# Pairing the two DMA queues of an HBM-to-HBM shift on the same rows instead of on diagonal quadrants

## The chip, the cores and the metric

One core of a Trainium2 chip. The metric is the device time in microseconds. Executions of the kernel before agree within some 0.2% on one chip. Kernels are compared only within the same rounds.

## The reference

```python
def setup_inputs():
    return {"x": np.random.randn(8192, 8192).astype(np.float32)}

def reference(x):
    return np.fft.ifftshift(x)
```

For even sizes this swaps the quadrants: `out[r, c] = x[(r + 4096) % 8192, (c + 4096) % 8192]`. 268.44 MB are read from HBM (the memory outside the core) and as many written to it; nothing is computed. A row is 32 KiB, a half row 16 KiB.

## The kernel before

```python
STEP = 8
# ... R, C = 8192; hr = hc = 4096
dims = [[STEP * C, hr // STEP], [1, hc]]          # 512 half rows, every eighth row
for c in range(STEP):
    for col in (0, hc):
        for eng, r0, h in ((nc.sync, 0, col), (nc.scalar, hr, hc - col)):
            eng.dma_start(
                out=bass.AP(out.tensor, out.offset + (r0 + c) * C + h, dims),
                in_=bass.AP(x.tensor, x.offset + (hr - r0 + c) * C + hc - h, dims),
            )
```

32 DMAs of 8 MiB, 16 on each of two queues, straight from HBM to HBM. At any time sync and scalar work in diagonal quadrants. The order on each queue is that of the program; the waits are in the prediction.

Of the kernel before, what the change touches and what calls it, by code (L numbers as in the profile page):

```python
# [1 line left out]

# [4 lines left out]


STEP = 8  # L10


@with_exitstack
def kernel(
    ctx: ExitStack,
    tc: tile.TileContext,
    x: bass.AP,
    out: bass.AP,
):



    nc = tc.nc

    R, C = x.shape
    hr = R // 2
    hc = C // 2

    dims = [[STEP * C, hr // STEP], [1, hc]]
    for c in range(STEP):  # L30
        for col in (0, hc):
            for eng, r0, h in ((nc.sync, 0, col), (nc.scalar, hr, hc - col)):
                eng.dma_start(
                    out=bass.AP(out.tensor, out.offset + (r0 + c) * C + h, dims),
                    in_=bass.AP(x.tensor, x.offset + (hr - r0 + c) * C + hc - h, dims),
                )


# [1 line left out]
_INS = ['x']  # L40
_OUTS = [((8192, 8192), 'float32')]


def kernel(**inputs):
    import numpy as _np
    import concourse.bacc as _bacc
    import concourse.tile as _tile
    from concourse import mybir as _mybir
    from concourse.bass_utils import run_bass_kernel_spmd as _run

    nc = _bacc.Bacc("TRN2", target_bir_lowering=False, num_devices=1)  # L51
    arrays, args = {}, []
    for name in _INS:
        a = _np.ascontiguousarray(inputs[name])
        if a.dtype.kind in "iu":
            a = a.astype(_np.int64)
        arrays[f"in_{name}_dram"] = a
        args.append(nc.dram_tensor(f"in_{name}_dram", a.shape, _mybir.dt.from_np(a.dtype), kind="ExternalInput").ap())
    for i, (shape, dtype) in enumerate(_OUTS):
        dt = _mybir.dt.from_np(_np.dtype(dtype))  # L60
        args.append(nc.dram_tensor(f"out_{i}_dram", shape, dt, kind="ExternalOutput").ap())
    with _tile.TileContext(nc) as tc:
        kernel(tc, *args)
    r = _run(nc, [arrays], core_ids=[0])
    got = tuple(r.results[0][f"out_{i}_dram"] for i in range(len(_OUTS)))
    return got[0]
```

## Time and profile before

| | before |
|---|---|
| median of the three runs | 822.29 us |
| mean / median packet | 801 / 773 ns |
| packets at the floor (up to 615 ns) | 26.2% |
| packets over 1,000 ns | 14.6% |
| lead of sync's queue over scalar's, mean and 5 to 95% (20 to 760 us) | 3.4 rounds, 2.6 to 3.9 |

A packet is one entry of the trace's packet records, here one half row. The last four rows are worked out from these records, which hold queue, start, duration and bytes of each packet. A "round" is 16 packets of one queue, on average one for each engine, and the lead is the number of packets started on sync's queue less those on scalar's, over 16. The page itself is read in the prediction. One more view belongs to it, the copy's line with its two issuing queues (ns that the issue instruction took, minimum, median and maximum; then first and last start in us):

```profile
L33 ACTq DMA_DIRECT2D out_dram<-in_x_dram x16: 518/42177/48098, 0.7 to 618.8; - x16
L33 SPq DMA_DIRECT2D out_dram<-in_x_dram x16: 511/41599/47782, 0.7 to 613.7; - x16
```

An issue instruction of 42 us looks busy. But the first three on each queue took 0.6 to 0.9 us in the trace, and only the fourth 43 us (sync) and 48 us (scalar). So I read the long ones as waiting for room behind DMAs that are already queued; no view names this wait.

### The profile page before, as it was taken

How to read it: one execution, taken by the hardware profiler on the slowest of the kernel's cores; microseconds unless marked ns; L12 is line 12 of the kernel's file. 1: busy time of each engine (PE TensorE's matmuls, PEld its weight loads, DVE VectorE, ACT ScalarE, POOL GpSimd, SP SyncE). 2: the span in 40 equal slices, each digit the busy share in tenths (PEclk: the TensorE clock that was granted, in tenths of full speed). 3: DMA queues.
4: the chain of work that ended last, by engine and by line, in shares of the span. 5: the costliest groups of instructions: out<-in, count | busy, mean ns of one | idle time of the engine just before them, and what ended most of it. 6: DMA issues, size and time to landing. Idle time of an engine off the chain costs nothing. (4 is left out here: it accounts for less than half of the span.)

```text
span 821.3 us, 77 instructions
## 1 busy us (share of the span) xinstructions
POOL 0.2 (0%) x4
## 2 busy tenths in 40 slices
POOL 0000000000000000000000000000000000000000
DMA  9999999999999999999999999999999999999998
GB/s 304 325 328 333 326 325 330 321 329 330 325 330 330 327 328 333 329 330 330 328 328 327 334 325 330 326 326 328 331 329 330 326 332 326 328 324 333 326 328 298
DMA packets 16896, 268.44 MB, mean 327 GB/s; under 512 B 512, under 2 KB 512, under 8 KB 512
## 3 DMA queue, kind: packets, MB, share of 16 engines
q1 hardware_dynamic: 8448, 134.22, 50.2%
q10 hardware_dynamic: 8448, 134.22, 49.7%
HBM read 268.44 MB, written 268.44 MB: 654 GB/s over the span
## 5 line engine op out<-in xcount | busy, mean ns | idle before, releaser
L51 POOL MEMSET const-bfloat16-1.0<- 128x1 bf16 x1 | 0.1, 103 | 0.0
L51 POOL MEMSET const-uint8-127<- 128x1 uint8 x1 | 0.1, 102 | 0.0
L51 POOL MEMSET const-float32-0.0<- 128x1 f32 x1 | 0.1, 99 | 0.2 <-issue 0.2
L51 POOL MEMSET const-float32-1.0<- 128x1 f32 x1 | 0.1, 99 | 0.0
## 6 DMA issues: line engine op xcount, KB each, us to landing
out_dram<-in_x_dram ACTq DMA_DIRECT2D x16, 8192.0 KB, 204.3
out_dram<-in_x_dram SPq DMA_DIRECT2D x16, 8192.0 KB, 204.1
```

The costliest lines, as they stand in the source:

```text
L51: nc = _bacc.Bacc("TRN2", target_bir_lowering=False, num_devices=1)
```

## The change

The intent: let both queues work on the two column halves of the same rows at the same time, so that what they touch lies side by side, 16 KiB apart.

```diff
-    for c in range(STEP):
-        for col in (0, hc):
-            for eng, r0, h in ((nc.sync, 0, col), (nc.scalar, hr, hc - col)):
+    for r0 in (0, hr):
+        for c in range(STEP):
+            for eng, h in ((nc.sync, 0), (nc.scalar, hc)):
                 eng.dma_start(
                     out=bass.AP(out.tensor, out.offset + (r0 + c) * C + h, dims),
                     in_=bass.AP(x.tensor, x.offset + (hr - r0 + c) * C + hc - h, dims),
```

## The prediction

> **What bounds the kernel now.** I read the page from the top: engines first, then the slices, then the DMA queues, then the issues.
>
> ```profile
> span 821.3 us, 77 instructions
> ...
> POOL 0.2 (0%) x4
> ...
> DMA  9999999999999999999999999999999999999998
> GB/s 304 325 328 333 326 325 330 321 329 330 325 330 330 327 328 333 329 330 330 328 328 327 334 325 330 326 326 328 331 329 330 326 332 326 328 324 333 326 328 298
> DMA packets 16896, 268.44 MB, mean 327 GB/s; under 512 B 512, under 2 KB 512, under 8 KB 512
> ...
> q1 hardware_dynamic: 8448, 134.22, 50.2%
> q10 hardware_dynamic: 8448, 134.22, 49.7%
> HBM read 268.44 MB, written 268.44 MB: 654 GB/s over the span
> ...
> out_dram<-in_x_dram ACTq DMA_DIRECT2D x16, 8192.0 KB, 204.3
> out_dram<-in_x_dram SPq DMA_DIRECT2D x16, 8192.0 KB, 204.1
> ```
>
> No compute engine works: 0.2 us on GpSimd in the whole span. All 16 DMA engines are full in every slice and the rate is flat, 321 to 334 GB/s between the first and last slice. The two queues have the same bytes and together take 99.9% of the engines' time. So the span is moved bytes over a sustained rate. The start and the end hold little:
>
> ```profile
> 0.00:20.00 20.00, 0.20 (x4) 1.00 0.91 301
> 20.00:200.00 180.00, 0.00 (x0) 1.00 1.00 328
> 200.00:400.00 200.00, 0.00 (x0) 1.00 1.00 329
> 400.00:600.00 200.00, 0.00 (x0) 1.00 1.00 328
> 600.00:800.00 200.00, 0.00 (x0) 1.00 1.01 328
> 800.00:821.00 21.00, 0.00 (x0) 1.00 0.92 304
> ```
>
> (Columns: stretch, length, GpSimd, clock, DMA share, GB/s.) At 328 GB/s all 268.44 MB would take 818.4 us, so the ends cost about 3 us.
>
> The next question is what one packet costs. The trace's packet records hold 16,384 data packets of 16,384 bytes, each one half row, so 1,024 on each of the 16 engines. Their mean is 801 ns: 1,024 x 801 ns = 820 us, which is the span. The shortest is 608 ns, and 26% lie within 615 ns; the median is about 775 and 15% take over 1,000. So 611 ns (26.8 GB/s an engine, 429 over sixteen) is what a packet costs when nothing stands in its way, and if all packets were like that the span would be 1,024 x 611 = 626 us. The other 190 ns of the mean packet are waiting outside the engine, and the memory is the only shared thing left: read and written together it carries 654 GB/s.
>
> Last, the issue side, because a queue that ran dry would look like slow packets.
>
> ```profile
> SPq L62 <- DMA out_dram<-in_x_dram: 167.2, 2, 118.8
> SPq L33 <- DMA out_dram<-in_x_dram: 133.8, 12, 50.6
> ```
>
> Sync waits at the copy's line 12 times: from its fifth DMA on, each waits for the one four places earlier (eight completion semaphores, four a queue). This costs nothing: a DMA lands 204 us after its issue while one lands per queue every 51 us, so four are always queued and the engines stay full.
>
> **What the Trainium skill says.** (1) "DMA: Bandwidth & Descriptors", section "Issuing engines are not separate DMA queues": DMAs from any issuing engine run on the same 16 engines and interleave. The section "Queues, rings and completion order" adds that an engine goes round its queues by packet. The trace agrees: 50.2 against 49.7%, and the two queues' packet counts stay within four rounds of 16 packets of each other all along. (2) "HBM Reference", "Specifications (TRN2)": about 716 GB/s for a domain of two cores. With 654 GB/s of reads and writes the trace stands at 91% of that, if both tensors lie in one domain, which no view here shows. (3) "DMA: Bandwidth & Descriptors", "Latency and other measured facts", on row pitch at large powers of two: copies between HBM tensors fall to 207 GB/s a direction at a pitch of 512 KiB and to 103 at 4 MiB. Here the pitch within a DMA is 8 rows x 32 KiB = 256 KiB and the trace has 327, so this DMA shape isn't hit that hard; but the table says that the placement of concurrent streams can matter a lot.
>
> **The change, part by part.** *Removed and added instructions:* none. On each engine the order and the waits of the changed program compare as the same: 16 DMAs a queue, each 512 rows of 4,096 floats, first four without a wait, the rest behind the one four places earlier. Cost: 0. *Packets:* 16,384 data packets of 16 KiB as before, the same alignment and pitch. Cost: 0. *Bytes:* the same 268.44 MB each way. Cost: 0. *What moves:* the addresses that the two queues have in work together. Before, sync and scalar sat in diagonal quadrants: different row halves and different column halves, on both the read and the write side, 128 MiB plus or minus 16 KiB apart. After, sync writes the left and scalar the right half of the same output rows, from the two halves of the same input rows, nominally 16 KiB apart. For the first half of the time all reads are from the lower half of x and all writes go to the upper half of out, then the reverse.
>
> So the whole effect must come through the 190 ns of waiting per packet. Two readings say that address relation matters little. First, before already contains variants: even DMAs of a queue have the one sign of the column offset and odd DMAs the other, and c runs from 0 to 7. Grouped in starting order, the mean packet of a DMA is 785 to 823 ns on q1 (sync, the queue that starts first) and 781 to 814 on q10 (scalar), with no alternation. Nor do the 32 positions inside a DMA show any repeated slow place. Second, "at the same time" isn't quite what the chip will do. Sync starts first, and its lead over scalar is 2 to 4 rounds all the way (landings of paired DMAs are 4.4 to 5.1 us apart, but for the last pair). A pair of rounds takes 2 x 0.80 = 1.6 us, so the other half row would be touched some 3 rows, or 5 us, later. Rows in a DMA are 256 KiB apart, so the actual distance between the two queues becomes about 3 x 256 KiB = 0.75 MiB, not 16 KiB. I expect the intended neighbourhood to be largely lost. Sum: 822.3 + 0 + 0 + 0, with an expected shift of the packet mean of 0 ns: 822 us.
>
> **The rivals.**
>
> *Locality wins.* If the second half row comes cheaper because its neighbour has just been read or written, waiting falls on half the packets. Suppose it takes 20% off the 190 ns for those: 0.5 x 38 = 19 ns, 1,024 x 19 = 19 us, giving 803 us. For it: the waiting is there to be won. Against: the lag of 5 us, and the 91% of the skill's domain figure; that figure as a ceiling would be 536.87 MB / 716 = 750 us, and I don't believe that a mix of reads and writes gets near all of it.
>
> *Crowding loses.* Halving the area in use at a time (one half of x read, one half of out written) could put more streams on the same parts of the memory. If waiting grows by a quarter, 190 x 0.25 = 48 ns, the span grows by 49 us to 871 us; by a tenth, 19 us to 841 us. For it: the skill's pitch table shows falls by two and more from placement alone; and the 15% of packets over 1,000 ns are collisions of some kind. Against: the flat rate, and that no DMA of before is worse than the others.
>
> *The queues drift apart or the waits bite.* If one queue runs ahead until its four DMAs are used up, the lag changes and the end has one queue alone. Round-robin held the lag to four rounds before, and a queue alone still fills its engine, so I give this under 2 us.
>
> **Range and chances.** The 2% borders are 806 and 839 us, that is a packet mean about 16 ns lower or higher than 801. The repeatability is 0.1% (821.98 to 822.63), so only a true shift gets there. The evidence inside the trace says no shift, but it can't show a relation that before never has (both queues in the same rows), and the pitch table warns. I take 65% for within 2%, 16% for faster (capped by the memory), 19% for slower (uncapped). The range 800 to 845 holds the small forms of both rivals; I predict 822 us.
>
> **What would show it.** Right: slices flat near 327 GB/s, packet mean near 801 ns with the same 611 ns floor and about 26% at it, queues at 50% each, the lag between queues still 2 to 4 rounds, and 204 us from issue to landing. Locality: floor share clearly above 26%, mean under 785 ns. Crowding: floor share lower and the share over 1,000 ns above 15%, or a rate that differs between the two halves of the run, when reads and writes change sides. The prediction fails if the memory's cost depends on which regions are read and written together rather than on bytes alone, or if the lag vanishes and neighbouring halves do meet.

## The result and the profile after

The changed kernel took 822.51 us (median of 6 runs, 822.23 to 822.97) beside 822.26 us of the kernel before (6 runs of the same rounds). The ratio is 1.0002, 95% interval 0.9989 to 1.0015: the same.

The page of the changed kernel, the lines that answer to those in the prediction:

```profile
span 820.6 us, 77 instructions
...
DMA  9999999999999999999999999999999999999998
GB/s 304 327 328 329 327 331 326 327 328 331 331 328 327 329 328 316 327 331 330 331 324 338 329 329 330 331 326 329 329 327 330 331 329 325 329 331 327 330 329 294
...
q1 hardware_dynamic: 8448, 134.22, 49.9%
q10 hardware_dynamic: 8448, 134.22, 49.7%
HBM read 268.44 MB, written 268.44 MB: 654 GB/s over the span
...
out_dram<-in_x_dram SPq DMA_DIRECT2D x16, 8192.0 KB, 204.0
out_dram<-in_x_dram ACTq DMA_DIRECT2D x16, 8192.0 KB, 203.9
```

Its time in stretches (stretch, length, GpSimd, clock, DMA share, GB/s), and sync's wait:

```profile
20.00:200.00 180.00, 0.00 (x0) 1.00 1.00 328
200.00:400.00 200.00, 0.00 (x0) 1.00 1.00 328
400.00:600.00 200.00, 0.00 (x0) 1.00 1.00 329
600.00:800.00 200.00, 0.00 (x0) 1.00 1.00 329
800.00:821.00 21.00, 0.00 (x0) 1.00 0.88 287
```

```profile
SPq L33 <- DMA out_dram<-in_x_dram: 133.0, 12, 50.7
```

Nothing has moved. The rate stays within 324 to 338 GB/s in all but one slice between the first and the last (316 in slice 16), the queues have half the time each, landing (the time from a DMA's issue to its completion) takes 204 us, sync waits 133.0 instead of 133.8 us. The stretches before and after 400 us, where reads and writes change sides of the tensors, have 328 and 329 GB/s. The packet records say the same: mean 798 ns (801 before), 28.2% at the floor (26.2), 14.2% over 1,000 ns (14.6). The lead of sync is again 3.4 rounds (2.6 to 3.9 in 90% of the time). So, by the order of the packets, the other half of a row is touched an estimated 3.4 x 2 x 0.80 = 5.4 us later, and meanwhile its queue has moved on by about 3 rows per engine.

### The profile page after: what moved, and what is told of

Read it like the earlier page. It is cut to its first block, busy times and chain, and to the rows that moved or that the text cites. A ratio compares the mean times of both kernels' runs of the same rounds, so it can differ in the third digit from the quotient of the medians.

```text
span 820.6 us, 77 instructions
## 1 busy us (share of the span) xinstructions
POOL 0.2 (0%) x4
## 2 busy tenths in 40 slices
DMA packets 16896, 268.44 MB, mean 327 GB/s; under 512 B 512, under 2 KB 512, under 8 KB 512
## 3 DMA queue, kind: packets, MB, share of 16 engines
HBM read 268.44 MB, written 268.44 MB: 654 GB/s over the span
```

## The experiments

The result leaves three theories. **A**: the relation between the queues does not matter; bytes and the sharing of the memory set the time. **B**: neighbouring halves would be cheaper together, but the lead of 5 us keeps them apart. **C**: halves that meet disturb each other, and the lead happens to prevent it. Under A there is a second question: are the 190 ns above the floor really something the engines share, and does placement ever matter?

All experiments but e10 are told here as edits of the changed kernel; the diffs are shortened, and "..." or a comment marks what is left out.

The expected times in us were set around the 822 us of the first rounds, but the runs fell on chips where the kernel before took 811.3 to 824.6 us. They are therefore read as ratios to the kernel before: "815 to 829" as within about 1%, "806" and "839" as 2% faster and slower. Read as bare times, e7's and e1's 811 to 812 us would lie outside theory A's range although the kernel before took just as long on that chip.

### e3_halves_meet: set sync back by 4 rounds

```diff
+    # sync first copies the last 4 rows per engine of its last DMA; then as before; the last DMA has 28
+    dims = [[32 * STEP * C, 16], [STEP * C, n], [1, hc]]      # n = 32, 4 or 28
+    copy(nc.sync, hr, STEP - 1, 0, first=28, n=4)
     for r0 in (0, hr): ...
```

> The changed kernel with the sync queue set back by 4 rounds (it first copies the last 4 rows per engine of its last DMA), so that the lead of 2 to 4 rounds that sync had is cancelled and both halves of a row are in work within about one round. Theory A (only the bytes count, the relation of the two queues does not matter): 822 us, between 815 and 829, share of packets at the 611 ns floor 24 to 30%. Theory B (neighbouring halves are cheaper together, but the lead of 5 us hid it): under 806 us and a floor share above 32%. Theory C (neighbouring halves disturb each other when they do meet): over 839 us.

Measured: 843.24 us (5 runs) beside 811.48 us on that chip, ratio 1.0405 (1.0379 to 1.0432). On its face that is theory C. The page shows otherwise (the last two lines give KB and us to landing):

```profile
span 839.1 us, 78 instructions
...
GB/s 245 330 332 333 334 329 333 336 333 332 332 336 336 333 329 335 332 334 333 336 327 333 330 329 337 332 337 330 334 327 334 334 330 331 332 336 315 216 206 173
...
out_dram<-in_x_dram SPq DMA_DIRECT2D x1, 7168.0 KB, 128.6
out_dram<-in_x_dram SPq DMA_DIRECT2D x1, 1024.0 KB, 16.2
```

```profile
740.00:760.00 20.00, 0.00 (x0) 1.00 1.02 338
...
780.00:800.00 20.00, 0.00 (x0) 1.00 1.03 224
800.00:820.00 20.00, 0.00 (x0) 1.00 0.98 206
```

From the second slice to the 36th the rate is 327 to 337 GB/s, no lower than elsewhere; the loss is all in the first slice and the last four. These are the stretches in which the small first and the last DMA of sync are in work. Only these two have kept the 16 x n form: in the trace the issue instructions carry 4 x 16 and 28 x 16 half rows for them, and 512 x 1 for all others (n = 32), so these were joined when the program was built. In the packet records the first DMA's 64 packets took 1,230 ns in the mean and the last one's 448 packets 1,584 ns, while scalar's packets, on the same engines in the last stretch, took 859 ns. And after the slow start the lead was turned round: sync's packet count ran 4.3 rounds behind, 8.3 by place in the row order. The middle of the run thus only shows one more distance of the queues at the usual rate; with the halves apart, it tested neither B nor C. e3 was a faulty control (its edit changed more than the one thing to be tested), and it pointed to something that does cost time, taken up in e9.

### e8_meet_again and e12_three_rounds: the control mended

```diff
-    dims = [[32 * STEP * C, 16], [STEP * C, n], [1, hc]]
+    dims = [[STEP * C, n], [1, hc]]            # n = 512, 64 or 448; e12: 512, 48 or 464
```

> e3_halves_meet mended: there the first and last sync DMA had a 16 x 4 and 16 x 28 form whose packets were slow (1230 and 1584 ns) while all other packets ran at the usual 790 ns, so that the 4% came from the control's own ends and not from halves that met. Here they are 64 and 448 rows in the same two-dimensional form as all others. Theory A (the relation of the queues does not matter): within 1% of before, flat slices. Theory C (halves that meet disturb each other): 3 to 5% slower again, as in e3. Theory B: over 2% faster.

Measured: 824.23 us (5 runs) beside 824.44, ratio 0.9996 (0.9983 to 1.0010).

```profile
span 822.5 us, 78 instructions
...
GB/s 301 324 330 329 323 330 327 331 327 327 331 326 329 327 332 327 323 330 325 329 326 327 328 324 327 331 327 331 321 329 331 328 331 326 331 327 328 326 329 296
...
out_dram<-in_x_dram SPq DMA_DIRECT2D x1, 7168.0 KB, 149.1
out_dram<-in_x_dram SPq DMA_DIRECT2D x1, 1024.0 KB, 7.0
```

The first DMA of 1,024 KB now lands after 7.0 us (16.2 in e3), the slices are flat to the end, and the 4% are gone. By place in the row order sync was 1.5 rounds behind scalar (0 to 2.0 at the extremes), where the changed kernel has it 3.4 ahead. I wanted it nearer still:

> e8 with sync set back by 3 rounds in place of 4. In e8 sync's packet count stayed 2.0 to 2.9 rounds ahead, so by place in the row order it was 1 to 2 rounds behind scalar; here it should be within 1 round, so that the two halves of a row are really in work at the same time. Theory A (the relation of the queues does not matter): within 1% of before. Theory B (locality, hidden by the lag): over 2% faster. Theory C (halves that meet disturb each other): over 2% slower.

Measured: 811.51 us (5 runs) beside 811.34, ratio 1.0001 (0.9988 to 1.0015). The aim was missed: the count's lead fell from 2.5 to 1.5 rounds along with the shift, so by place sync was again 1.5 rounds behind. The queues thus ran at a distance of +3.4 and of -1.5 rounds (2.4 us) without any difference in time, so C falls for these distances. A distance of zero that lasts was not reached by any run and stays open.

### e7_full_rows: the two halves one after the other in one queue

```diff
-    dims = [[STEP * C, hr // STEP], [1, hc]]
+    half = hr // STEP // 2
     # loops and calls shortened
-    for r0 ...: for c ...: for eng, h in ((nc.sync, 0), (nc.scalar, hc)):
+    for c ...: for part in range(2): for eng, r0 in ((nc.sync, 0), (nc.scalar, hr)):
+        row = c + part * half * STEP
-        out ... dims,  in_ ... dims
+        out=bass.AP(..., (r0 + row) * C,           [[STEP * C, half], [hc, 2], [1, hc]]),
+        in_=bass.AP(..., (hr - r0 + row) * C + hc, [[STEP * C, half], [-hc, 2], [1, hc]]),
```

> Each DMA copies 256 whole rows as pairs of half rows one after the other in the same queue (the read side steps backwards by half a row), sync for the upper, scalar for the lower half of the output. The two halves of a row follow each other in one engine, at most two packets apart. Theory A (only bytes count): 815 to 829 us. Theory B (locality of the row pays when it is really met): under 806 us. Theory C: over 839 us.

Measured: 811.48 us (5 runs) beside 811.48, ratio 0.9999 (0.9986 to 1.0011), 22.3% of packets at the floor.

```profile
HBM read 268.44 MB, written 268.44 MB: 664 GB/s over the span
```

Here the neighbourhood does not depend on the lead at all: by the access pattern, the next packet of the same queue is the other half of the row (the trace shows the form 256 x 2 half rows, but no addresses). It gains nothing. Theory B falls for halves that follow each other in a queue.

### e4_one_queue: no second queue

```diff
-            for eng, h in ((nc.sync, 0), (nc.scalar, hc)):
+            for eng, h in ((nc.sync, 0), (nc.sync, hc)):
```

> The changed kernel with all 32 DMAs on the sync queue, left and right halves in turn; no second queue that could stand in any relation to it. If the time is bytes over a memory rate: 815 to 829 us, packet mean near 801 ns. If having two address streams open at once costs something: under 806 us. If two queues are needed to keep the engines full: over 839 us with a DMA share under 0.97.

Measured: 823.85 us (4 runs) beside 824.55, ratio 0.9991 (0.9974 to 1.0007); packet mean 798 ns.

```profile
q1 hardware_dynamic: 16896, 268.44, 99.5%
```

One queue carries everything and keeps the engines full. With the relation taken away entirely the time stays. This is the most direct support for A: there is no pairing left that could be good or bad.

### e5_eight_engines: are the 190 ns shared?

```diff
-    dims = [[STEP * C, hr // STEP], [1, hc]]
+    wide = hr // 8
+    dims = [[wide * C, 8], [STEP * C, wide // STEP // 2], [1, hc]]
     ...  # for each c and queue 2 DMAs of 4 MiB, from row c + part * wide // 2
```

> The same packets, but the outermost size is 8, so that each DMA uses 8 engines in place of 16 (if it does, each moves 2,048 packets). If the 190 ns of waiting per packet come from what the sixteen engines share, they mostly go: packet mean 611 to 650 ns, 1250 to 1330 us, most packets at the floor. If they belong to a copy within an engine or its path, the mean stays near 800 ns and the time is about 1640 us.

Measured: 1253.83 us, one run. The page:

```profile
span 1252.0 us, 109 instructions
...
DMA  4555555555555555555555555555555555555554
...
HBM read 268.44 MB, written 268.44 MB: 429 GB/s over the span
```

Half the engines are busy, as the Trainium skill has it ("DMA: Bandwidth & Descriptors", section "Why a DMA increments its semaphore by 16 and not by 1": the outermost size decides how many engines a DMA uses, the largest number up to 16 that divides it on both sides). 99.2% of the packets are at the floor and the mean is 612 ns: 2,048 x 612 = 1,253 us. The copy of half a row costs an engine 611 ns when eight of them work; with sixteen it costs 801. So the waiting comes from what the sixteen share; whether that is the memory or the way to it, this run does not say.

### e11_stores_only and e6_scalar_to_sbuf: reads, writes, or both

```diff
+    held = ...tile([128, 4, hc])   # filled once from x
     ... for eng, h in ((nc.sync, 0), (nc.scalar, hc)):
-                    in_=bass.AP(x.tensor, ...),
+                    in_=held[:],
```

> Wrong result on purpose: one tile is read once and all 256 MiB of output are written from it, so HBM is written and hardly read. If the writes alone set the copy's rate: packet mean near 800 ns, about 830 to 850 us with the load at the start. If reads and writes together do: packets near the 611 ns floor, 640 to 680 us.

Measured: 656.95 us, one run (wrong result). The page's packets and HBM traffic:

```profile
span 655.2 us, 78 instructions
...
DMA packets 17424, 276.83 MB, mean 423 GB/s; under 512 B 528, under 2 KB 528, under 8 KB 528
...
HBM read 8.39 MB, written 268.44 MB: 423 GB/s over the span
```

The packet mean is 617 ns. Writing alone goes at the engines' own pace: 428 GB/s from 200 to 400 us. So writes alone do not set the copy's 327 GB/s.

```diff
     ... nc.scalar in place of the copy of the right half:
+                sink = pool.tile([128, 4, hc])      # two buffers, 8 MiB each
+                nc.scalar.dma_start(out=sink[:], in_=x half rows)
```

> Wrong result on purpose: scalar's half of the rows is read into the on-chip buffer and not written to HBM; all 16 engines move as many packets, HBM carries three quarters of the bytes. If the HBM traffic sets the waiting: 403 MB at 654 GB/s would be 616 us, under the floor of 626 us, so 640 to 700 us with a floor share above 50%. If the waiting comes from the engines or their path and not from HBM: 800 to 830 us.

Measured: 717.23 us, one run (wrong): 17 us above the first range, so a miss in time, though 66.3% of the packets are at the floor as that range asked, and far from the second. The stretches (columns as above) show why one number does not describe it:

```profile
200.00:300.00 100.00, 0.00 (x0) 1.00 1.00 344
300.00:400.00 100.00, 0.00 (x0) 1.00 1.00 348
...
600.00:700.00 100.00, 0.00 (x0) 1.00 1.01 429
```

Scalar had only two buffers and fell behind, so the first part was mostly copy and the end was mostly, from about 600 us wholly, load. The end shows reads alone at 429 GB/s, again the engines' pace. In the stretch from 200 to 300 us the packet records give sync 260 GB/s of copy and scalar 84 of load: 2 x 260 + 84 = 604 GB/s of HBM traffic, less than the copy's 654, with all engines busy. "HBM bytes over one fixed rate" is therefore too simple: the mix, or the placement of the loads (a form of 128 x 4 half rows), counts too. Which of them was not separated.

### e1_rows_contiguous and e2_pitch_4mib: does placement matter inside a DMA?

```diff
-    dims = [[STEP * C, hr // STEP], [1, hc]]        # row c, c + 8, ...
+    dims = [[C, hr // STEP], [1, hc]]               # e1: 512 neighbouring rows, from row 512 * c
+    dims = [[C, 16], [16 * STEP * C, 32], [1, hc]]  # e2: 16 rows side by side, then 4 MiB on, from row 16 * c
```

> The changed kernel with each DMA on 512 neighbouring rows in place of every eighth row: pitch 32 KiB, engines presumably 1 MiB apart in place of 8 MiB. Theory A in its strict form (placement never matters, bytes alone): 815 to 829 us. Theory A in its weak form (placement matters within a DMA, among the 16 engines, but not between the two queues): a time outside 806 to 839 us, in either direction.

Measured: 811.96 us (4 runs) beside 811.48, ratio 1.0017 (0.9985 to 1.0049). The time did not change. The packets did somewhat: 34.7% at the floor and 16.0% over 1,000 ns in the profiled run, which was the longest of the four (817.61 us).

> The changed kernel with the 16 engines on 16 neighbouring rows and a step of 128 rows (4 MiB) from packet to packet of an engine; the same number of DMAs, packets and bytes. Strict form of theory A: 815 to 829 us. Weak form: outside 806 to 839 us; if the Trainium skill's table on row pitch (103 GB/s a direction at 4 MiB) carries over to it, up to 2600 us.

Measured: 820.56 us (4 runs) beside 811.48, ratio 1.0111 (1.0098 to 1.0125): 1.1% slower, clear of noise but far from the 103 GB/s that the skill gives at that pitch (page and section in the prediction). The profile's page:

```profile
HBM read 268.44 MB, written 268.44 MB: 655 GB/s over the span
```

If, as the access pattern suggests, the outer 16 is shared out over the engines, steps of 4 MiB from packet to packet in one engine do little harm while the engines lie side by side. e1 fits the strict form of theory A; e2 lies between the two forms, over 1% but under 2%. The strict form falls with e9, below.

### e9_spread_same_rows and e10_spread_diagonal: what was slow in e3

```diff
+    wide = hr // 16
+    dims = [[wide * C, 16], [STEP * C, 16], [1, hc]]
     ...  # for each c and queue 2 DMAs of 4 MiB, from row c + part * wide // 2
```

e9 has the changed kernel's pairing, e10 the pairing of the kernel before.

> The changed kernel's pairing of queues, with each DMA cut in two of 256 rows in the 16 x 16 form, in which each engine should stay in its own block of 256 rows (8 MiB from the next engine's). If the placement of the 16 engines in one DMA is what made those packets of e3 slow: packet mean 1200 to 2500 ns, 1250 to 2500 us. If they were slow for another reason (the ends of the run, a smaller DMA, one queue's last DMA): 815 to 840 us.

> The kernel before's diagonal pairing in the same 16 x 16 form as e9. Theory A, that the relation of the two queues never matters: the same time as e9 within 2%. Its rival, that the relation matters once placement binds: a difference from e9 of over 5%, in either direction.

Measured: e9 1688.34 us, e10 1709.97 us, one run each, beside 824.44 us of the kernel before on that chip. First e9's page, then e10's:

```profile
span 1686.6 us, 109 instructions
...
DMA  9999999999999999999999999999999999999999
...
HBM read 268.44 MB, written 268.44 MB: 318 GB/s over the span
```

```profile
HBM read 268.44 MB, written 268.44 MB: 314 GB/s over the span
```

The engines are as full as ever and move half: packets of 1,632 ns in the mean in e9, 12% at the floor. So the same rows in the same number of 16 KiB packets take twice as long when, by the access pattern, the 16 engines keep 8 MiB from each other. The form with an outer 16 is not itself slow, since e2 has it too, and neither are 4 MiB DMAs with 256 KiB steps, since e5 has those at the floor, with 8 engines. Which rows one DMA has in work together matters by a factor of two. That it is the distance of the engines is read from the access pattern, and distance alone is not enough: e5's eight engines stand 16 MiB apart by theirs and run at the floor. And in this form the pairing of the queues moves 1.3% (1709.97 over 1688.34, one run each, so no interval), within the 2% that e10's expectation allowed theory A.

A consequence that is argued, not shown, and that speaks against the "8 MiB" which e1's expectation presumed for the changed kernel: two such DMAs cover the same 512 rows that one DMA of the kernel before covers. If that one gave each engine a block of 32 of its rows, the engines would lie 8 MiB apart there as well and it should be as slow. So it probably shares its rows out in another way. The trace records no addresses, so which way stays open.

## Why the prediction was right

- **The bound.** The step "1,024 packets x 801 ns is the span" holds wherever the engines are full: 798 ns gives the changed kernel, 612 with 2,048 packets gives e5, and 617 gives e11 (16,896 packets with the load, so 1,056 an engine, x 617 = 652 us, beside a span of 655 us).
- **"The other 190 ns are waiting outside the engine", in something shared.** Shown by e5: gone with eight engines. Reads alone and writes alone do not bring it about: in the end of e6 and in e11 they go at 429 and 428 GB/s. But there HBM also carries fewer bytes than in a copy, so these two do not separate the mixing from the amount; only e6's 604 GB/s speaks against the amount alone. The prediction's next step, that the memory is the only shared thing left, was not shown. That the same packets take twice as long in e9 says only that the waiting depends on the addresses.
- **No instructions, packets or bytes differ.** The page after has 77 instructions, 16,896 packets and 268.44 MB, as before.
- **The lead of 2 to 4 rounds remains**, 3.4 in the mean both times, so the halves do not meet as intended. This was right as a description, but it was not needed as a cause: e7, e8 and e12 brought the halves closer together by the order of the packets and e4 removed the second queue, without gain or loss.
- **Rival of locality.** Its supposed 20% off the waiting of half the packets did not come even in e7, where each half row directly follows its neighbour in a queue.
- **Rival of crowding.** The changed kernel shows none. The warning that the prediction took from the skill's pitch table was sound in general, as e9 shows, but in the runs here it concerns the rows within a DMA. The passage cut from the prediction took the table's 207 GB/s at 512 KiB for a fall; the page calls 214 full for its copies, so only its rows from 2 MiB on are falls, and the 327 measured here lies above all of them. What the prediction calls the placement of concurrent streams is the page's explanation of the table, which the page itself calls an unverified inference. The change leaves that form as it was, and e10 against e9 says that the pairing is small beside it.
- **Rival of drifting queues.** The lead stayed between 2 and 4 rounds, and one queue alone fills the engines (e4).
- **The signs.** The floor share was a poor one: on one chip it was 22.3% in e7, 24.2% in e12, 28.4% in e2 and 34.7% in e1, and of these e2 was the slowest. The mean packet is what goes with the time.

What the prediction did not foresee: with 19% for slower it placed the danger in the relation between queues, while the sensitive place lay untouched beside it.

## What to carry to other kernels

When every DMA engine is busy in every slice, compare the mean packet with the shortest: the difference may be what sharing costs, and a run on half the engines (as e5) shows whether it really is shared. Reordering which queue takes which block did nothing here while the packets' number and size and each DMA's access pattern stayed the same; try instead which rows the outermost dimension of an access pattern puts next to each other (e2 against e9). And when a control comes out slow, find in its slices where the loss lies before it is counted for a theory: e3's 4% were all in the stretches of its own first and last DMA.

## What the Trainium skill lacked or had wrong

- "HBM Reference", "Specifications (TRN2)" and "Access": no figure for copies within HBM by one core (the DMA page has one, next point). Here loads alone ran at 429 GB/s and stores alone at 428, but a copy at 327 each way, 654 together (663 and 664 in e12 and e7, on another chip), with the engines full yet not at their own pace.
- "DMA: Bandwidth & Descriptors", "Latency and other measured facts": the row pitch entry calls 214 GB/s a direction full for its copies between HBM tensors; here they reached 327, on another chip 332. It gives 103 GB/s at 4 MiB without saying which dimension of a larger pattern that means. By the access patterns, steps of 4 MiB inside the outer 16 kept 327 (e2), while an outer step of 8 MiB with inner steps of 256 KiB fell to 159 (e9).
- The same page, "The descriptor swizzle": says which engine takes which partition for 128 partitions, not how 512 rows from HBM to HBM are shared out. The factor of two between e9 (1,688 us) and the kernel before (824 us) may hang on that.
- No page has the spread between chips: the same kernel took 811.3 to 811.5 us on chip 4, 824.4 on chip 1 and 824.6 on chip 6, and 822.3 in the rounds of the result. That is 1.6% at most, more than any pairing of queues did.
